# Scan layer: six convolution tiles projected in 512-column matmuls over both halves of x

## The chip, the core and the metric

The kernel runs on one core of a Trainium2 chip. Five engines of that core matter here: PE (TensorE, the matmuls), DVE (VectorE), ACT (ScalarE), POOL (GpSimd) and SP, which issues most of the transfers. Each engine works through its own list of instructions in order and waits on semaphores where an instruction needs another engine's result. The metric is the device time of one execution in microseconds (us); smaller is better. Three runs of the kernel before lie between 1007.13 and 1008.31 us.

## What is computed

The whole kernel is a decoder trunk of two layers on 256 tokens with 1024 channels. Each layer is FFN, mixer, FFN, with a layer norm after each; the first layer's mixer is a sparse attention, the second's a scan (SSD). The change lies in the scan mixer alone, in its beginning:

```python
def ssd_mixer(x, w_in, conv_w, conv_b, dt_bias, a_log, d_skip, norm_g, w_out):
    z, xbc, dt = jnp.split(x @ w_in, [SSM_INNER, SSM_INNER + SSM_CONV_DIM], axis=-1)
    xbc_pad = jnp.pad(xbc, ((0, 0), (SSM_CONV - 1, 0), (0, 0)))
    conv = conv_b + xbc_pad[:, 0:seq] * conv_w[0]
    for k in range(1, SSM_CONV):
        conv = conv + xbc_pad[:, k:k + seq] * conv_w[k]
    xbc = jax.nn.silu(conv)
    xs, b_in, c_in = jnp.split(xbc, [SSM_INNER, SSM_INNER + SSM_GROUPS * SSM_STATE], axis=-1)
    ...
    y = ssd_scan(xs, dt, a, b_in, c_in)
```

`xbc` has 3072 columns: 2048 of xs (four groups of 512), 512 of B and 512 of C. All arithmetic is float32 in effect.

## The kernel before

**Split products.** The matmuls run in a rounded 32-bit format. To keep float32 accuracy a weight block is split into a high part `wh` (ACT casts it, line 326) and a low part `wl` (DVE subtracts the high part from the raw weights, line 354; for a few blocks ACT and a transfer of POOL make it, lines 332 and 333). The activations `xT` are split likewise and lie side by side in one tile, `xT.HL`: for each of eight blocks of 128 channels 256 columns of the high half `xT.H`, then 256 of the low half `xT.L`. A product is the sum of three: high by high, high by low, low by high.

**A convolution tile.** The 3072 columns are worked as 24 tiles of 128 channels by 256 tokens. `bc_tile` (line 1508) makes the four B tiles and the four C tiles, `xs_tile` (line 1622) those of the four groups of xs. Each calls `proj_b` (line 691), which issues 24 matmuls of 256 columns (lines 539, 540 and 541 in `mm3`, for eight blocks) into the first half of one PSUM bank, and then `conv` (line 1497):

- ACT writes `a` = bias + last tap times the bank (line 1500);
- `flush` lets ACT take the Silu of the tile before (line 1495), held back by one tile so that ACT need not wait for DVE;
- DVE adds the three other taps, each a SCALAR_TENSOR_TENSOR that reads the bank (line 1504);
- the tile's own Silu is put in the list `late` for the next call.

After that `W.pump` makes the next weight block or two: a cast on ACT, a subtraction on DVE. The bank comes from `xbank` (line 1460), three banks in turn.

**The order of the work.** It is written out by hand, at the end of `ssd`: the eight B and C tiles, with the cumulative sums of the decay behind the sixth (`cumsums`, line 1420: five small matmuls; then ACT loads its table for Exp, takes two exponentials and loads the table for Silu again); the four xs tiles of group 0, with `cb` behind the second; then `flush`, half of a z product (`z_half`, line 1466), `x_tok(0)`, and the groups.

In this document the tiles around the change are called C0 to C3 (the four C tiles) and X0 to X3 (group 0 of xs). Two places on PE need what `conv` made:

- `cb(0)`, `cb(1)` and `cb_cross` (lines 1519 to 1535), behind X1: three times four small matmuls on B and C, one for each head group (the profile counts each of them twice). Those of the fourth head group read C3's Silu. DVE then masks two results (line 1533, `cbm`) and ACT copies the third (line 1526, `cross`).
- `x_tok(0)` (line 1565), behind X3 and the z half: eight transposes (line 1570) of X0 to X3. The fourth reads X3's Silu.

`proj_w` (line 700) is used elsewhere, in the FFN (`one`, line 914): for each of the eight blocks one matmul of the high weights with all 512 columns of `xT.HL` (line 705), then for each block one of the low weights with the 256 high columns (line 707). The bank then holds high by low in its second half and the other two sums in its first; there ACT copies the second half out (line 929) and DVE adds the first to it (line 930).

Of the kernel before, what the change touches and what calls it, by code (L numbers as in the profile page):

```python
# [18 lines left out]
SEQ = 256  # L19
# [393 lines left out]
def trunk_kernel(ctx: ExitStack, tc: tile.TileContext, widths, forms, x, ln_g, ln_b, wts, kvg, convp,  # L413
                 dt_bias, a_log, d_skip, norm_g, out):
    nc = tc.nc
# [10 lines left out]
    def nm(s):  # L426
        cnt[0] += 1
        return f"{s}_{cnt[0]}"
# [7 lines left out]
    def f1(s):  # L436
        return wk.tile([128, 256], F32, name=nm(s), tag="f1", bufs=6)
# [10 lines left out]
    def pmm():  # L448
        return psum.tile([128, 512], F32, name=nm("pmm"), tag="pmm", bufs=2)
# [14 lines left out]
    W = Weights(nc, f4, ring, wts, widths, forms, SLOTS, RAWS)  # L464
# [73 lines left out]
    def mm3(ps, lh, ll, rh, rl, first, last, on=False):  # L538
        nc.tensor.matmul(ps, lh, rh, start=first, stop=False, skip_group_check=on)  # L539
        nc.tensor.matmul(ps, lh, rl, start=False, stop=False, skip_group_check=on)  # L540
        nc.tensor.matmul(ps, ll, rh, start=False, stop=last, skip_group_check=on)  # L541
# [149 lines left out]
    def proj_b(ps, xT, u, retire=True):  # L691

        H, L = W.get(u)
        for k in range(DK):
            c = slice(k * 128, (k + 1) * 128)
            mm3(ps, H[:, c], L[:, c], xT.H[:, k, :], xT.L[:, k, :], k == 0, k == DK - 1)
        if retire:
            W.retire(u + 1)

    def proj_w(ps, xT, u):  # L700


        H, L = W.get(u)
        for k in range(DK):
            nc.tensor.matmul(ps, H[:, k * 128:(k + 1) * 128], xT.HL[:, k, :], start=k == 0, stop=False)  # L705
        for k in range(DK):
            nc.tensor.matmul(ps[:, :SEQ], L[:, k * 128:(k + 1) * 128], xT.H[:, k, :], start=False, stop=k == DK - 1)
        W.retire(u + 1)

    def out_k(acc, t, lh, ll, u, first, last):  # L710
        H, L = W.get(u)
# [53 lines left out]
    def ffn(xT, u0, ln_i, first=False, last=False, ff=False, own=1, k1=5, mixer=False):  # L765
# [148 lines left out]
        def one(j):  # L914

            nonlocal u
            bank = pmm if j % 2 == 0 else ptr
            if j % 2 == 0:
                hH[j // 2], hL[j // 2] = r2("hH"), r2("hL")
            H, L = [a[j // 2][:, (j % 2) * 256:(j % 2 + 1) * 256] for a in (hH, hL)]  # L920
            g, h = f1("gate"), f1("h")

            def half(o):
                nonlocal u
                ps = bank()
                proj_w(ps, xT, u)
                W.product()
                u += 1
                nc.scalar.copy(o, ps[:, SEQ:])
                return lambda: nc.vector.tensor_add(o, ps[:, :SEQ], o)  # L930

            def mul():
                nc.vector.tensor_mul(h, h, g)
                W.owe(1400)
                later(lambda: nc.scalar.copy(H, h))
                later(lambda: nc.vector.tensor_sub(L, h, H.bitcast(F32)), 2)

            later(half(g))
            step(most=-1, plain=True)
            later(lambda: nc.scalar.activation(g, g, AF.Silu))  # L940
            later(half(h))
            later(mul, 2)
            step(most=-1, plain=True)
# [436 lines left out]
    def ssd(xT, u, ln_i):  # L1380
# [79 lines left out]
        def xbank():  # L1460

            turn[0] += 1
            return psum.tile([128, 512], F32, name=nm("pxs"), tag=("acc00", "acc01", "acc10")[turn[0] % 3], bufs=1)
# [29 lines left out]
        def flush():  # L1493
            while late:
                nc.scalar.activation(*late.pop(0), AF.Silu)

        def conv(ps, i, out_t, hold=False):
            w = convp_sb
            a = f1("cv")
            nc.scalar.activation(a, ps[:, :256], AF.Identity, bias=w[:, 4, i:i + 1], scale=w[:, 3, i:i + 1])  # L1500
            if not hold:
                flush()
            for s in range(1, 4):
                nc.vector.scalar_tensor_tensor(a[:, s:], ps[:, :256 - s], w[:, 3 - s, i:i + 1], a[:, s:],
                                               op0=ALU.mult, op1=ALU.add)
            late.append((out_t, a))

        def bc_tile(i):
            ps = xbank()
            proj_b(ps[:, :256], xT, u + 10 + i, False)  # L1510
            W.free(u + 10 + i)
            dst = bT if i < 4 else cTt
            conv(ps, 16 + i, dst[:, (i % 4) * 256:(i % 4 + 1) * 256])
            W.pump(1 + i % 2)

        cbm = f4("cbm")
# [105 lines left out]
        def xs_tile(g, i, uu, then=None):  # L1622
            if not i:
                xsT[g] = []
            ps = xbank() if g < 3 else pmm()
            proj_b(ps[:, :256], xT, uu, False)
            W.free(uu)
            o = wk.tile([128, 256], F32, name=nm("xsT"), tag="xsT", bufs=5)
            hold = g == 3 and then is not None
            conv(ps, g * 4 + i, o, hold)  # L1630
            xsT[g].append(o)
            if then:
                then()
            if hold:
                nc.scalar.activation(*late.pop(0), AF.Silu)
            W.pump(1)
# [30 lines left out]
        for i in range(8):  # L1667
            bc_tile(i)
            if i == 5:
                cumsums()  # L1670
                for t in range(2):
                    decay_load(t, 0)
        u += 18
        for i in range(4):
            xs_tile(0, i, u + i)
            if i == 1:
                cb(0)
                cb(1)
                cb_cross()
# [11 lines left out]
        for g in range(2):  # L1691
            v = u + 8 * g
            fill += [lambda g=g, i=i, v=v: xs_tile(g + 1, i, v + i, first_diag if (g, i) == (0, 2) else None)
                     for i in range(4)]
            fill += [lambda g=g, t=t, i=i, v=v: (z_half(g + 2, t, i, v + 4), t and i and decay(g + 1), W.pump(1))
                     for t in range(2) for i in range(2)]
        v = u + 16
        fill += [lambda i=i, k=k, x=x, v=v: xs_tile(3, k, v + i, (lambda: run2(1)) if k == 1 else None) if x else out_piece(k, v + i)
                 for i, (x, k) in enumerate(((1, 0), (1, 1), (0, 0), (1, 2), (1, 3), (0, 1), (0, 2), (0, 3)))]
        fill += [lambda i=i, v=v: out_piece(4 + i, v + 8 + i) for i in range(6)]  # L1700
# [72 lines left out]
    xT = XT(True)  # L1773
    u, xT = ffn(xT, 0, 0, first=True, mixer=True)
    u, xT = attention(xT, u, 1)
    u, xT = ffn(xT, u, 2, ff=True)
    u, xT = ffn(xT, u, 3, own=3, k1=4, mixer=True)
    u, xT = ssd(xT, u, 4)
    u, _ = ffn(xT, u, 5, last=True)
# [36 lines left out]
```

## Time and profile before

| | |
|---|---|
| median of 3 runs | 1007.43 us (1007.13 to 1008.31) |
| the profiled execution's own time | 1007.07 us |
| its span, first to last instruction | 1005.4 us |
| mean granted TensorE clock | 0.998 of full speed |
| PE busy in the span | 996.3 us (99%) |
| DVE busy | 903.4 us (90%) |
| ACT busy | 667.6 us (66%) |
| POOL busy | 110.7 us (11%) |
| mean DMA rate | 231 GB/s |
| stretch of the tiles C0 to X3 | about 668 to 698 us |

Each row of a timeline has the start of an instruction (or of a run of like ones) in us from the span's start, its duration, the engine, the line of the kernel, the operation with its output and inputs, and, in square brackets, how long the engine was idle before and what ended that. A run of n like instructions has "xn" behind it. Instructions of one engine overlap a little: what one costs its engine in a row of others is the distance to the next start. For matmuls this matters most, since their durations include the way through the array: a 256-column one is shown with 0.28 us, and the next starts 0.12 us later.

### The profile page before, as it was taken

How to read it: one execution, taken by the hardware profiler on the slowest of the kernel's cores; microseconds unless marked ns; L12 is line 12 of the kernel's file. 1: busy time of each engine (PE TensorE's matmuls, PEld its weight loads, DVE VectorE, ACT ScalarE, POOL GpSimd, SP SyncE). 2: the span in 40 equal slices, each digit the busy share in tenths (PEclk: the TensorE clock that was granted, in tenths of full speed). 3: DMA queues.
4: the chain of work that ended last, by engine and by line, in shares of the span. 5: the costliest groups of instructions: out<-in, count | busy, mean ns of one | idle time of the engine just before them, and what ended most of it. 6: DMA issues, size and time to landing. Idle time of an engine off the chain costs nothing.

```text
span 1005.4 us, 14633 instructions
## 1 busy us (share of the span) xinstructions
PE 996.3 (99%) x5305; PEld 842.1 (84%) x5305; DVE 903.4 (90%) x1222; ACT 667.6 (66%) x978; POOL 110.7 (11%) x151
## 2 busy tenths in 40 slices
PE   9999999999999999999999999999999999999997
PEld 6888888898788888888888888999888888888886
DVE  6899999889898999999899999788899988899996
ACT  6676776576755776764577776486778645676670
POOL 0010110100000101100010110251121110010100
PEclk9999999999999999999999999999999999999999
DMA  9699889651754998995499999657765754689981
GB/s 348 218 291 279 242 262 327 225 170 63 236 180 126 273 271 236 272 383 199 125 273 274 240 266 358 208 163 237 229 212 200 256 173 139 181 251 288 288 255 42
DMA packets 66343, 232.74 MB, mean 231 GB/s; under 512 B 8144, under 2 KB 9168, under 8 KB 66272
## 3 DMA queue, kind: packets, MB, share of 16 engines
q1 hardware_dynamic: 54288, 189.84, 51.9%
q0 software_dynamic: 11408, 41.46, 22.4%
q8 instruction: 41, 0.67, 0.3%
q10 hardware_dynamic: 576, 0.52, 0.2%
q14 instruction: 30, 0.25, 0.1%
HBM read 193.48 MB, written 1.08 MB: 194 GB/s over the span
## 4 chain that ended last, share of the span: by engine, by line
PE 97%; DMA 1%; DVE 1%; ACT 0%; issue 0%; DVEq 0%; ACTq 0%; SPq 0%
PE pmm L539 13%; PE pmm L541 13%; PE pmm L540 13%; PE acc L539 10%; PE acc L541 10%; PE acc L540 10%; PE ptr L540 2%; PE ptr L541 2%; PE ptr L539 2%; PE pxs L539 2%; PE pxs L540 2%; PE pxs L541 2%; PE pmm L705 1%; PE ptr L705 1%; PE ptr L797 1%; DMA raw<-in_wts_dram 1%
## 5 line engine op out<-in xcount | busy, mean ns | idle before, releaser
L354 DVE TENSOR_TENSOR wl<-raw,wh 128x1024 fp32r<-128x1024 f32 (+3 forms) x422 | 493.3, 1212 | 15.1 <-ACT wh L326 14.8
L326 ACT CAST wh<-raw 128x1024 fp32r<-128x1024 f32 (+2 forms) x431 | 428.9, 1043 | 94.9 <-DVE raw L293 49.1
L539 PE MATMUL acc<-wh,hH 128*128 128x512 f32 (+1 forms) x352 | 138.2, 393 | 0.0
L541 PE MATMUL acc<-wh,hL 128*128 128x512 f32 (+1 forms) x352 | 136.7, 388 | 0.0
L540 PE MATMUL acc<-wl,hH 128*128 128x512 f32 (+1 forms) x352 | 136.4, 388 | 0.0
L539 PE MATMUL pmm<-wh,xT 128*128 128x512 f32 (+2 forms) x304 | 118.9, 391 | 0.0
L541 PE MATMUL pmm<-wh,xT 128*128 128x512 f32 (+2 forms) x304 | 116.8, 384 | 0.0
L540 PE MATMUL pmm<-wl,xT 128*128 128x512 f32 (+2 forms) x304 | 116.6, 384 | 0.0
L266 POOL DMA_DIRECT2D raw<-raw x64 | 55.6, 869 | 490.6 <-DVE raw L293 261.0
L541 PE MATMUL pmm<-wh,xf 128*128 128x512 f32 x256 | 99.7, 390 | 0.0
L540 PE MATMUL pmm<-wl,xf 128*128 128x512 f32 x256 | 99.7, 389 | 0.0
L539 PE MATMUL pmm<-wh,xf 128*128 128x512 f32 x256 | 99.7, 389 | 0.0
L541 PEld LDWEIGHTS acc<-wh,hL 128*128 128x128 f32 x352 | 66.1, 188 | 13.6
L293 DVE TENSOR_TENSOR raw<-raw,raw 128x1024 f32<-128x1024 f32 x64 | 77.1, 1220 | 0.2
L540 PEld LDWEIGHTS acc<-wl,hH 128*128 128x128 f32 x352 | 66.2, 188 | 13.0
L539 PEld LDWEIGHTS acc<-wh,hH 128*128 128x128 f32 x352 | 66.2, 188 | 12.9
L541 PEld LDWEIGHTS pmm<-wh,xT 128*128 128x128 f32 x304 | 57.1, 188 | 11.6 <-DVE xT L536 0.2
L540 PEld LDWEIGHTS pmm<-wl,xT 128*128 128x128 f32 x304 | 57.2, 188 | 10.3 <-DVE wl L354 0.2
L539 PEld LDWEIGHTS pmm<-wh,xT 128*128 128x128 f32 x304 | 57.2, 188 | 10.0
L540 PEld LDWEIGHTS pmm<-wl,xf 128*128 128x128 f32 x256 | 48.1, 188 | 10.0
L539 PEld LDWEIGHTS pmm<-wh,xf 128*128 128x128 f32 x256 | 48.1, 188 | 10.0
L541 PEld LDWEIGHTS pmm<-wh,xf 128*128 128x128 f32 x256 | 48.1, 188 | 9.9
(338 smaller groups left out, 1785.1 us busy)
## 6 DMA issues: line engine op xcount, KB each, us to landing
raw<-in_wts_dram SPq DMA_DIRECT2D x338, 512.0 KB, 5.9
raw<-raw POOLq DMA_DIRECT2D x64, 512.0 KB, 5.7
M<-scr POOLq DMA_DIRECT2D x8, 512.0 KB, 6.5
wl<-raw POOLq DMA_DIRECT2D x7, 512.0 KB, 7.2
lng<-in_ln_g_dram SPq DMA_DIRECT2D x6, 512.0 KB, 5.1
lnb<-in_ln_b_dram SPq DMA_DIRECT2D x6, 512.0 KB, 5.6
raw<-in_wts_dram SPq DMA_DIRECT2D x4, 408.0 KB, 5.7
out_dram<-x SPq DMA_DIRECT2D x4, 256.0 KB, 2.1
```

The lines of the kernel that those rows point to most:

```text
L266: self.nc.gpsimd.dma_start(self.raw[r], self.raw[other], accum_op=ALU.add)
L293: self.nc.vector.tensor_add(self.raw[r], self.raw[r], self.raw[other])
L326: nc.scalar.copy(h[:, c:c + n], raw[:, c:c + n])
L354: self.nc.vector.tensor_sub(lo[:, s], raw[:, s], h[:, s].bitcast(F32))
L539: nc.tensor.matmul(ps, lh, rh, start=first, stop=False, skip_group_check=on)
L540: nc.tensor.matmul(ps, lh, rl, start=False, stop=False, skip_group_check=on)
L541: nc.tensor.matmul(ps, ll, rh, start=False, stop=last, skip_group_check=on)
L705: nc.tensor.matmul(ps, H[:, k * 128:(k + 1) * 128], xT.HL[:, k, :], start=k == 0, stop=False)
L797: nc.tensor.transpose(v[:, i, t * 128:(t + 1) * 128], hs[t][:, i * 128:(i + 1) * 128], ident)
```

## The change

`proj_w` gets a parameter so that it can leave the retiring of the weights to its caller. `conv` gets a parameter `wide`. Six tiles use both: C1, C2, C3 (`i > 4` in `bc_tile`) and X0, X1, X2 (`not g and i < 3` in `xs_tile`). For them `proj_w` fills a whole bank, with 8 matmuls of 512 columns and 8 of 256 in place of 24 of 256. `conv` then begins with an ACT copy of the bank's second half into the tile's output place, the flush of the tile before, and a DVE addition of the bank's first half; from there on the bias line (ACT) and the three taps (DVE) read that sum in SBUF, not the bank. All other tiles stay as they were.

```diff
-    def proj_w(ps, xT, u):
+    def proj_w(ps, xT, u, retire=True):
...
-        W.retire(u + 1)
+        if retire:
+            W.retire(u + 1)
...
-        def conv(ps, i, out_t, hold=False):
+        def conv(ps, i, out_t, hold=False, wide=False):
             w = convp_sb
             a = f1("cv")
+            if wide:
+                nc.scalar.copy(out_t, ps[:, SEQ:])
+                flush()
+                nc.vector.tensor_add(out_t, ps[:, :SEQ], out_t)
+                ps = out_t
             nc.scalar.activation(a, ps[:, :256], AF.Identity, bias=w[:, 4, i:i + 1], scale=w[:, 3, i:i + 1])
             if not hold:
                 flush()
...
         def bc_tile(i):
             ps = xbank()
-            proj_b(ps[:, :256], xT, u + 10 + i, False)
+            wide = i > 4
+            (proj_w if wide else proj_b)(ps if wide else ps[:, :256], xT, u + 10 + i, False)
             W.free(u + 10 + i)
             dst = bT if i < 4 else cTt
-            conv(ps, 16 + i, dst[:, (i % 4) * 256:(i % 4 + 1) * 256])
+            conv(ps, 16 + i, dst[:, (i % 4) * 256:(i % 4 + 1) * 256], wide=wide)
...
             ps = xbank() if g < 3 else pmm()
-            proj_b(ps[:, :256], xT, uu, False)
+            wide = not g and i < 3
+            (proj_w if wide else proj_b)(ps if wide else ps[:, :256], xT, uu, False)
...
-            conv(ps, g * 4 + i, o, hold)
+            conv(ps, g * 4 + i, o, hold, wide)
```

On DVE, from the two weight subtractions behind C0's tile to the second tap of C2, the list before has this (`wl` is a low weight part, `cv` the tile's running sum, `pxs` the bank, `at` and `nacs` what DVE takes from the cumulative sums):

```order
L354 TENSOR_TENSOR wl_6625<-raw_6542,wh_6624 128x1024 [waits DMAHW5_49,PE_49]
L354 TENSOR_TENSOR wl_6628<-raw_6583,wh_6627 128x1024 [waits DMAHW6_49,PE_49]
L1504 SCALAR_TENSOR_TENSOR cv_6697<-pxs_6672,convp_sb,cv_6697 128x255 [waits Activation_49]
L1504 SCALAR_TENSOR_TENSOR cv_6697<-pxs_6672,convp_sb,cv_6697 128x254 [waits DVE_49]
L1504 SCALAR_TENSOR_TENSOR cv_6697<-pxs_6672,convp_sb,cv_6697 128x253 [waits DVE_49]
L1430 COPY at_6716<-ptr_6708 32x256 [waits PE_49,Activation_49]
L1434 TENSOR_SCALAR nacs_6719<-ptr_6708 128x32
L1434 TENSOR_SCALAR nacs_6721<-ptr_6708 128x32
L1504 SCALAR_TENSOR_TENSOR cv_6752<-pxs_6727,convp_sb,cv_6752 128x255 [waits Activation_49]
```

and now, at the same place (line 1504 is the new addition here, 1510 the taps):

```order
L354 TENSOR_TENSOR wl_6625<-raw_6542,wh_6624 128x1024 [waits DMAHW5_49,PE_49]
L354 TENSOR_TENSOR wl_6628<-raw_6583,wh_6627 128x1024 [waits DMAHW6_49,PE_49]
L1504 TENSOR_TENSOR cTt_6242<-pxs_6672,cTt_6242 128x256 [waits Activation_49]
L1510 SCALAR_TENSOR_TENSOR cv_6689<-cTt_6242,convp_sb,cv_6689 128x255 [waits Activation_49]
L1510 SCALAR_TENSOR_TENSOR cv_6689<-cTt_6242,convp_sb,cv_6689 128x254 [waits DVE_49]
L1510 SCALAR_TENSOR_TENSOR cv_6689<-cTt_6242,convp_sb,cv_6689 128x253 [waits DVE_49]
L1431 COPY at_6710<-ptr_6702 32x256 [waits PE_49,Activation_49]
L1435 TENSOR_SCALAR nacs_6713<-ptr_6702 128x32
L1435 TENSOR_SCALAR nacs_6715<-ptr_6702 128x32
L1504 TENSOR_TENSOR cTt_6242<-pxs_6721,cTt_6242 128x256 [waits Activation_49]
L1510 SCALAR_TENSOR_TENSOR cv_6738<-cTt_6242,convp_sb,cv_6738 128x255 [waits Activation_49]
```

An addition stands ahead of the taps of each wide tile, behind the weight subtractions of the tile before, and both the addition and the first tap wait for ACT.

On ACT, from C1's tile to C2's, the list before has this (`dend` and `eacs` are the exponentials of the cumulative sums, `cTt` takes the Silu of the C tiles):

```order
L1500 ACTIVATE cv_6697<-pxs_6672,convp_sb 128x256 [waits PE_49]
L1495 ACTIVATE cTt_6242<-cv_6655 128x256 [waits DVE_49,Activation_49]
L326 CAST wh_6705<-raw_6622 128x1024 [waits DMAHW0_49]
L1427 ACT_TABLE_LOAD
L1427 ACTIVATE dend_6239<-ptr_6708 128x32 [waits PE_49]
L1428 ACTIVATE eacs_6240<-ptr_6708 128x32
L1500 ACTIVATE cv_6752<-pxs_6727,convp_sb 128x256 [waits PE_49]
L1495 ACT_TABLE_LOAD [waits DVE_49]
```

and now:

```order
L1502 COPY cTt_6242<-pxs_6672 128x256 [waits PE_49]
L1496 ACTIVATE cTt_6242<-cv_6655 128x256 [waits DVE_49,Activation_49]
L1506 ACTIVATE cv_6689<-cTt_6242,convp_sb 128x256 [waits DVE_49]
L326 CAST wh_6699<-raw_6622 128x1024 [waits DMAHW0_49]
L1428 ACT_TABLE_LOAD
L1428 ACTIVATE dend_6239<-ptr_6702 128x32 [waits PE_49]
L1429 ACTIVATE eacs_6240<-ptr_6702 128x32
L1502 COPY cTt_6242<-pxs_6721 128x256 [waits PE_49]
L1496 ACT_TABLE_LOAD [waits DVE_49]
L1496 ACTIVATE cTt_6242<-cv_6689 128x256 [waits Activation_49]
L1506 ACTIVATE cv_6738<-cTt_6242,convp_sb 128x256 [waits DVE_49]
```

The bias line (1506) now stands behind the Silu of the tile before, and it waits for DVE where it waited for PE; the cast and the table loads stand behind it.

## The prediction

> **What bounds the kernel now.** I read the page first. The span, and the shares of the chain of work that ended last:
>
> ```profile
> span 1005.4 us, 14633 instructions
> ...
> PE 97%; DMA 1%; DVE 1%; ACT 0%; issue 0%; DVEq 0%; ACTq 0%; SPq 0%
> ```
>
> The end is set by PE, so a time saved on PE is gained, and a time that PE waits is lost. The waits of PE come next; the longest in the whole span:
>
> ```profile
> PE ptr L492 <- DVE half L483: 1.2, 1, 1.2
> ```
>
> That is at the very start. Where the change lies PE waits for nobody. How near the others are to it is seen in the busy times of the stretches around the six tiles (columns: PE, PEld, DVE, ACT, POOL, then granted clock and DMA share):
>
> ```profile
> 675.00:687.00 12.00, 12.00 (x101) 11.85 (x100) 11.32 (x21) 10.79 (x17) 2.67 (x4) 1.00 0.81 216
> 687.00:699.00 12.00, 12.00 (x95) 11.46 (x93) 8.57 (x15) 7.11 (x14) 0.88 (x1) 1.00 0.82 255
> ```
>
> In the first, from C2 to X1, DVE has 0.68 us of 12 left and ACT 1.21. That is the number that matters most here: a change that gives both of them more to do has almost no cover.
>
> Then the timelines. PE's: one tile (X1), the twelve `cb` products behind it, and the transposes of `x_tok(0)`:
>
> ```profile
> 684.11 0.28 PE L539 MATMUL pxs<-xT,wh 128*128 128x256 f32 x1
> ...
> 686.99 1.06 PE L1532 MATMUL psp<-cTt,bT 128*128 128x128 f32 x8
> 687.89 1.06 PE L1532 MATMUL pmm<-cTt,bT 128*128 128x128 f32 x8
> ...
> 698.18 0.60 PE L1570 MATMUL py<-ident,xsT 128*128 128x128 f32 x4
> ```
>
> A tile takes 686.99 - 684.11 = 2.88 us, a set of four `cb` products 0.90. ACT's timeline from C1's cast to C2's, then the two Silus on which PE depends, C3's at 684.78 and X3's at 697.84:
>
> ```profile
> 675.59 1.04 ACT L326 CAST wh<-raw 128x1024 fp32r<-128x1024 f32 x1
> 676.64 1.28 ACT L1427 ACT_TABLE_LOAD   x1
> 677.93 0.20 ACT L1427 ACTIVATE dend<-ptr 128x32 f32<-128x32 f32 x1
> ...
> 678.55 0.56 ACT L1500 ACTIVATE cv<-pxs,convp_sb 128x256 f32<-128x256 f32 x1 [0.33 <-PE pxs L541]
> 679.14 1.28 ACT L1495 ACT_TABLE_LOAD   x1
> 680.43 0.42 ACT L1495 ACTIVATE cTt<-cv 128x256 f32<-128x256 f32 x1
> 680.75 1.03 ACT L326 CAST wh<-raw 128x1024 fp32r<-128x1024 f32 x1
> ...
> 684.78 0.41 ACT L1495 ACTIVATE cTt<-cv 128x256 f32<-128x256 f32 x1
> ...
> 697.84 0.42 ACT L1495 ACTIVATE xsT<-cv 128x256 f32<-128x256 f32 x1 [0.40 <-DVE cv L1504]
> ```
>
> C3's Silu ends at 685.19, and its readers start about 687.3 (the fourth of the set at 686.99): 2.1 us of cover. X3's ends at 698.26, when the transposes have begun and the fourth comes next: no cover at all.
>
> **PE's part.** A wide tile is priced by `proj_w` in the FFN:
>
> ```profile
> 846.26 1.98 PE L705 MATMUL pmm<-xT,wh 128*128 128x512 f32 x8
> 848.07 1.11 PE L707 MATMUL pmm<-xT,wl 128*128 128x256 f32 x8
> 849.04 2.11 PE L705 MATMUL pmm<-xT,wh 128*128 128x512 f32 x8
> ```
>
> 849.04 - 846.26 = 2.78 us, 0.10 under the 2.88. The columns streamed are the same 6144; only the cost of each instruction goes down. Six tiles would save 0.6 us. That is all that the change can gain.
>
> **The additions.** Six copies on ACT and six additions on DVE. The first row has ACT's price from the FFN, the others DVE's, from the groups with shapes kept apart:
>
> ```profile
> L929 ACT COPY gate<-pmm 128x256 f32<-128x256 f32 x4 | 1.5, 374 | 3.3 <-PE pmm L707 3.3
> ```
>
> ```profile
> L1504 DVE SCALAR_TENSOR_TENSOR cv<-pxs,convp_sb,cv 128x254 f32<-128x254 f32 x20 | 9.6, 482 | 0.7
> ...
> L1128 DVE SCALAR_TENSOR_TENSOR sc<-ridx,lt,sc 128x256 f32<-128x256 f32 x7 | 3.4, 485 | 0.3
> ...
> L930 DVE TENSOR_TENSOR gate<-pmm,gate 128x256 f32<-128x256 f32 x4 | 1.7, 418 | 0.0
> ```
>
> A copy is 0.37, an addition 0.42. The taps now read SBUF: line 1128 does the same operation from SBUF in 0.485 against 0.482 from the bank, so they keep their price. [...] The bias line from SBUF has no row of its own; I keep 0.56, and allow 0.1 either way.
>
> Beside the busy time comes a **new round trip**. Before, ACT's bias line waited for PE alone and could run while DVE was still at the weights; DVE found it ready. Now the addition stands in DVE's list behind the weight subtractions, ACT's bias line waits for it, and the taps wait for the bias line. In that time both engines stand still for each other, in every tile. DVE's list for a tile is addition, wait, taps, subtraction. The last two, and the masking behind `cb`, from DVE's timeline:
>
> ```profile
> 675.04 2.35 DVE L354 TENSOR_TENSOR wl<-raw,wh 128x1024 fp32r<-128x1024 f32 x2
> 677.31 1.51 DVE L1504 SCALAR_TENSOR_TENSOR cv<-pxs,convp_sb,cv 128x255 f32<-128x255 f32 x3
> 678.74 0.40 DVE L1430 COPY at<-ptr 32x256 f32<-32x256 f32 x1
> ...
> 689.88 0.69 DVE L1533 TENSOR_TENSOR cbm<-psp,tri 128x512 f32<-128x512 f32 x1 [0.57 <-PE pmm L1524]
> 690.48 0.68 DVE L1533 TENSOR_TENSOR cbm<-pmm,tri 128x512 f32<-128x512 f32 x1
> ```
>
> From start to start: a subtraction 1.14 (2.27 for two), three taps 1.43, a masking 0.60. For each handing over between engines I take 0.04, a choice that the range doubles. A tile's cycle is then addition 0.42 + 0.04, bias 0.56 + 0.04, taps 1.43, subtraction 1.14 = 3.63 us, where PE gives a new tile every 2.78.
>
> **The sum, step by step** (span time). C1's taps start at 677.31 in the trace, held by the two subtractions; its addition now starts there. Bias 677.77 to 678.33. Behind it stand ACT's cast (1.05 to the next start), the table load (1.29) and the two exponentials (0.2), so C2's copy comes at 680.87 and ends at 681.24; Silu's table 681.28 to 682.57, C1's Silu 0.32, C2's bias 682.89. Its taps 683.49, subtraction 684.92, C3's addition 686.06, bias 686.52, taps 687.12 (done 1.51 later), C3's Silu 688.67 to 689.08.
>
> PE comes to `cb` at 686.99 less five tiles' saving, 686.5, and has done three of the four head groups by 687.2 (0.90 for four). It waits until 689.1: **first wait, 1.9 to 2.2 us**.
>
> On DVE: C3's taps end by 688.55, subtraction, X0's addition 689.69, X1's 693.32 (one cycle). X1's part has the two maskings (1.20) in place of a subtraction: X2's addition 697.01. Its taps 698.07, subtraction 699.50, X3's taps 700.64 (its bias line, from the bank as before, is ready by then), Silu 702.19 to 702.61. Before it ended at 698.26: the transposes come 4.35 us later. From `cb` to the transposes PE worked 698.18 - 686.99 = 11.19 us; after its first wait it has that to do less the 0.68 done and the 0.10 saved on X2, and is there at 699.5. With the three transposes that it can do first (some 0.3) that makes a **second wait, some 2.9 us**. The two waits, 4.8 to 5.1, less the 0.6 saved make the same 4.2 to 4.5. The saving itself is lost: a PE that comes earlier only waits longer.
>
> Overlaps on ACT (a start comes up to 0.1 us before the end of the one before) take 0.2 off between C1 and C2: 4.1 to 4.35. I take **4.2**.
>
> What else moves. Casts behind the bias line come up to 4 us later, but each block is cast ahead: the one that is held at 678 belongs to the second tile of the next group, eight tiles on. Loads wait for raw tiles that DVE's subtractions set free, so they come as much later as the casts that need them, with the DMA share at 0.82. POOL and SP get no instruction. Banks come free with the addition: C2's at 681.7, well ahead of X1 at 683.7. After `x_tok(0)` everything is shifted alike, and PE sets the pace again, as the 97% say; nothing gives the 4.2 back.
>
> From the profiled execution's 1007.07 us that is 1011.3. The median of the runs shown is 1007.43, 0.36 above it, so 1011.6 against that; I predict 1011.5.
>
> **Rivals.**
> *Hidden, or a small gain.* The copies and additions fit beside PE and the 0.6 us is gained: 1006.8. For it: in 687 to 699 DVE has 3.4 us idle. Against it: the 0.68 us before that, and that the round trip cannot be filled by an engine that works its list in order. It holds only if a tile's cycle stays at 2.78 or below, or C3's Silu ends by 687.2 and X3's by 697.6, 5 us earlier than I work out. 0.10; this is the one on the other side.
> *Cheaper taps.* If a tap from SBUF took what the addition takes, 0.42 and not 0.48, fifteen taps in the chain (C2 to X2) give 0.9 back: 1010.6. [...] Rows 1128 and 1504 speak against it. 0.10.
> *A slower clock after the waits.* The granted clock is 1.00 in the windows here, but none of them has a PE idle for more than 1.2 us. If it halved for one tile after each wait, the first loss would vanish in the second wait, and the second would cost 2.9: 1014.4. [...] 0.05.
> *Half of it.* One of the two waits comes out much shorter, because DVE finds a bias line ready that I have as late: about 1009.4. 0.05.
>
> **How the numbers follow.** About 0.2%, 2.0 us, can be told from no change. The forecast has 0.70, and with the cheaper taps, the slower clock and most of the half case it makes slower by over 0.2% 0.88; same 0.10 (most of the hidden case, and the part of the half case that falls short of 1009.4); faster by over 0.2% 0.02, a rest of the hidden case, since 0.6 us is all that I see to gain. The range holds the forecast with its unknown prices (bias line 0.1 in five tiles, 0.5; handing over doubled in ten places, 0.4, on both sides together 0.9) and the cheaper taps with them: 1009.6 to 1013.0. It leaves out the hidden, the slower-clock and the half case, 0.20.
>
> **What would show it.** Right: in the profile after, PE idle in front of the `cb` products with ACT's `cTt` Silu as releaser, and again in front of the x_tok transposes with `xsT`, 2 to 3 us each; DVE idle some 0.6 us in each wide tile between addition and taps, with ACT's bias line as releaser; ACT idle until DVE's addition; additions 3.6 us apart from C3 on; wide tiles 2.8 us on PE. Wrong: PE without gaps between 670 and 705, or taps well under 0.48, or a PE that waits at a third place, for a weight or a bank.

## The result, and the profile after

| | before | after |
|---|---|---|
| median of the runs compared (6 each) | 1007.64 us | 1013.07 us |
| lowest to highest | 1007.13 to 1008.31 us | 1012.43 to 1014.00 us |
| ratio, 95% interval | | 1.0054 [1.0044, 1.0064] |
| profiled execution, its span | 1007.07 us, 1005.4 us | 1013.86 us, 1012.1 us |
| mean granted TensorE clock | 0.998 | 0.996 |

The change costs 5.4 us. The forecast was 1011.5 us with a range up to 1013.0; the median lies 0.07 us above that upper end.

The chain of work that ended last, from the page of after, has DVE and ACT in it now:

```profile
PE 88%; DVE 6%; DMA 2%; ACT 2%; issue 2%; POOL 0%; DVEq 0%; ACTq 0%; SPq 0%; POOLq 0%
```

The longest waits of PE in after (us in total, times, longest):

```profile
PE py L1577 <- ACT xsT L1496: 2.2, 1, 2.2
PE psp L1539 <- ACT cTt L1496: 1.8, 1, 1.8
PE ptr L492 <- DVE half L483: 1.2, 1, 1.2
PE pmm L685 <- ACT wh L326: 0.6, 1, 0.6
```

The first two are new, and they stand where the prediction put them: `cb` (line 1539) waits for C3's Silu, the transposes (line 1577) for X3's. The last is a start-up wait that before has too, shorter. PE's timeline of after shows the wide tiles and both waits:

```profile
679.11 2.00 PE L705 MATMUL pxs<-xT,wh 128*128 128x512 f32 x8
...
681.90 2.00 PE L705 MATMUL pxs<-xT,wh 128*128 128x512 f32 x8
...
690.08 0.49 PE L1539 MATMUL psp<-cTt,bT 128*128 128x128 f32 x2 [1.76 <-ACT cTt L1496]
...
700.61 0.85 PE L1577 MATMUL py<-ident,xsT 128*128 128x128 f32 x3
703.69 0.33 PE L1577 MATMUL py<-ident,xsT 128*128 128x128 f32 x1 [2.24 <-ACT xsT L1496]
703.86 0.60 PE L1577 MATMUL ptr<-ident,xsT 128*128 128x128 f32 x4
704.22 0.38 PE L539 MATMUL pxs<-xT,wh 128*128 128x256 f32 x1
704.41 0.39 PE L540 MATMUL pxs<-xT,wh 128*128 128x256 f32 x1
704.61 0.41 PE L541 MATMUL pxs<-xT,wl 128*128 128x256 f32 x1
```

A wide tile takes 681.90 - 679.11 = 2.79 us. The last rows hold something not foreseen: from 704.41 on the 256-column matmuls start 0.20 to 0.22 us apart, where it is 0.12 elsewhere. The windows of this stretch show why (columns: PE, PEld, DVE, ACT, POOL busy, granted clock, DMA share, GB/s):

```profile
700.00:704.00 4.00, 1.62 (x10) 1.03 (x9) 3.89 (x7) 2.54 (x5) 0.00 (x0) 1.00 0.33 56
704.00:705.00 1.00, 1.00 (x9) 1.00 (x7) 1.00 (x2) 0.98 (x2) 0.00 (x0) 0.71 0.85 291
705.00:706.00 1.00, 1.00 (x7) 1.00 (x6) 1.00 (x3) 0.99 (x2) 0.00 (x0) 0.50 1.04 418
...
707.00:708.00 1.00, 1.00 (x7) 1.00 (x7) 1.00 (x3) 0.00 (x0) 0.00 (x0) 0.58 0.07 20
708.00:709.00 1.00, 1.00 (x10) 1.00 (x10) 1.00 (x2) 0.04 (x1) 0.00 (x0) 1.00 0.00 0
```

The granted clock falls to 0.50 shortly after the second wait and comes back before 708. In the 40 slices of the profile's page, some 25 us each, no such stretch can be seen; only the mean, 0.996 for 0.998, hints at it.

**Where the 6.7 us of span went.** The same matmul in both traces, each ahead of, between or behind the places in question. In before:

```profile
644.25 0.49 PE L557 MATMUL ptr<-ident,x 128*128 128x128 f32 x3
...
698.61 0.60 PE L1570 MATMUL ptr<-ident,xsT 128*128 128x128 f32 x4
...
707.77 0.44 PE L1585 MATMUL ptr<-M,xdt 128*64 128x128 f32 x4
...
819.40 0.38 PE L557 MATMUL pxT<-ident,x 128*128 128x128 f32 x2
```

and in after:

```profile
645.19 0.38 PE L557 MATMUL ptr<-ident,x 128*128 128x128 f32 x2
...
714.52 0.44 PE L1592 MATMUL ptr<-M,xdt 128*64 128x128 f32 x4
...
826.15 0.49 PE L557 MATMUL pxT<-ident,x 128*128 128x128 f32 x3
```

At 645, ahead of every changed tile, after is already 645.19 - 644.25 = 0.94 us late. This is no part of the change: 0.36 is there at line 685's matmuls of the start (11.12 for 10.76), and ahead of 645 this execution has two more waits of PE of 0.2 us each that the one of before has not (line 540 for `wl`, line 557 for DVE's `x`). The fourth transpose comes at 703.69 for about 698.5 (the set of four starts at 698.18, the next one at 698.61), 5.2 late, so 4.25 from the two waits. At the next common matmul the lag is 714.52 - 707.77 = 6.75: another 1.56 in a stretch in which nobody waits and the clock is at half. From there it stays at 6.75 (826.15 against 819.40).

### The profile page after: what moved, and what is told of

Read it like the earlier page. It is cut to its first block, busy times and chain, and to the rows that moved or that the text cites. A ratio compares the mean times of both kernels' runs of the same rounds, so it can differ in the third digit from the quotient of the medians.

```text
span 1012.1 us, 14544 instructions
## 1 busy us (share of the span) xinstructions
PE 998.2 (99%) x5257; PEld 841.0 (83%) x5257; DVE 905.6 (89%) x1228; ACT 670.5 (66%) x984; POOL 110.5 (11%) x151
## 4 chain that ended last, share of the span: by engine, by line
PE 88%; DVE 6%; DMA 2%; ACT 2%; issue 2%; POOL 0%; DVEq 0%; ACTq 0%; SPq 0%; POOLq 0%
PE pmm L539 12%; PE pmm L540 12%; PE pmm L541 12%; PE acc L539 9%; PE acc L541 9%; PE acc L540 9%; DVE wl L354 3%; PE ptr L539 2%; PE ptr L541 2%; PE ptr L540 2%; PE pmm L705 1%; PE ptr L705 1%; PE ptr L798 1%; DVE cv L1510 1%; DMA raw<-raw 1%
```

## The experiments

All eight were compared with the kernel before on the same chip in the same hours. In the first four that one took 1007.76 us (13 runs, 1007.27 to 1008.30), in the last four 1007.64 us (33 runs, 1006.93 to 1008.88). The edits are to the kernel after, but for the fourth.

**1. The round trip taken away, the work kept.** The bias line reads the bank's first half and stands ahead of the addition, so that ACT waits for PE alone again. Copies, additions and wide matmuls stay. The bias line's tap leaves out the high-by-low products in the six tiles.

```diff
             if wide:
                 nc.scalar.copy(out_t, ps[:, SEQ:])
+            nc.scalar.activation(a, ps[:, :256], AF.Identity, ...)
+            if wide:
                 flush()
                 nc.vector.tensor_add(out_t, ps[:, :SEQ], out_t)
                 ps = out_t
-            nc.scalar.activation(a, ps[:, :256], AF.Identity, ...)
```

> Copy and addition stay in the six wide tiles, but ACT's bias line reads the bank's first half at once, ahead of the flush, and does not wait for DVE's addition. (So the last tap of these tiles leaves out the high-by-low products.) Theory, the round trip: DVE finds the bias line ready, its cycle falls from 3.63 to about 3.0 us, C3's Silu comes before PE needs it and X3's within some 0.5 us: no wait of 2 us on PE, no fall of the clock, 1007.0 to 1008.2 us. Rival, the added work itself (0.42 us of DVE and 0.37 of ACT in each tile where both were nearly full): the waits stay for the most part, 1010 us or more.

Measured: 1007.78 us (10 runs, 1007.35 to 1009.75), ratio 1.0003 [0.9993, 1.0013]. Both new waits are gone from PE's list, and DVE runs without a gap from C1's addition to the maskings behind `cb`. A part of its timeline:

```profile
683.76 0.42 DVE L1506 TENSOR_TENSOR cTt<-pxs,cTt 128x256 f32<-128x256 f32 x1
684.21 1.52 DVE L1511 SCALAR_TENSOR_TENSOR cv<-cTt,convp_sb,cv 128x255 f32<-128x255 f32 x3
685.65 1.22 DVE L354 TENSOR_TENSOR wl<-raw,wh 128x1024 fp32r<-128x1024 f32 x1
686.79 0.42 DVE L1506 TENSOR_TENSOR xsT<-pxs,xsT 128x256 f32<-128x256 f32 x1
```

From addition to addition it is 3.03 us, for the same instructions. The copies and additions, less what PE saves in the wide matmuls, change nothing that can be measured in the medians; the 5.4 us come with the waiting. The trace says a little more: from the transposes at 645 to the first product with `M` this kernel takes 63.29 us and before 707.77 - 644.25 = 63.52. So some 0.2 of the half microsecond that PE saves is left, and the other 0.3 is what six copies and additions still cost.

**2. PE kept busy through the second wait.** Nine 512-column matmuls whose result nobody reads, in front of `x_tok(0)`.

```diff
         z_half(1, 1, 1, uz)
+        pb = pmm()
+        for _ in range(9):
+            nc.tensor.matmul(pb, xT.HL[:, 0, :128], xT.HL[:, 0, :], start=True, stop=True)
         x_tok(0)
```

> The changed kernel with nine extra matmuls of 512 columns, whose result is not used, between the z half and the transposes of x_tok(0): PE has 2.0 us of work in the wait of 2.24 us. Theory, the clock falls because PE stood still: the granted clock stays at 1.00 from 703 to 708 us and the time falls by about 1.5 us, to 1011.4 to 1011.9. Rival, the 6.7 us in the span come from waits alone or from another place: no change, 1012.8 to 1013.4 us.

Measured: 1012.17 us (4 runs, 1011.99 to 1012.61), ratio 1.0044 [1.0029, 1.0059]: 0.3 above the span that I gave, in the median. PE's second wait is 0.5 us, and the stretch in which after has the half clock is at full clock here:

```profile
704.00:705.00 1.00, 1.00 (x9) 1.00 (x10) 1.00 (x2) 0.98 (x2) 0.00 (x0) 1.00 1.00 295
705.00:706.00 1.00, 1.00 (x10) 1.00 (x10) 1.00 (x2) 0.99 (x2) 0.00 (x0) 1.00 0.96 373
```

The added work runs in time that PE would have waited: the fourth transpose comes 58.50 us after the transposes at 645, as in after (703.69 - 645.19 = 58.50). What is left, 1012.17 - 1007.76 = 4.4 us, is the two places where PE has to wait. So the half clock hangs on PE's idleness there (0.5 us of wait in place of 2.24), not on what DVE and ACT do; nor do transfers explain it, since the DMA share is 1.00 and 0.96 here at full clock.

**3. The round trip without the wide matmuls.** The six tiles go back to 24 matmuls in half a bank; a copy and a DVE operation of the same cost stay (a maximum of the first half with its copy, which gives the same numbers).

```diff
-                nc.scalar.copy(out_t, ps[:, SEQ:])
+                nc.scalar.copy(out_t, ps[:, :SEQ])
                 flush()
-                nc.vector.tensor_add(out_t, ps[:, :SEQ], out_t)
+                nc.vector.tensor_max(out_t, ps[:, :SEQ], out_t)
...
-            (proj_w if wide else proj_b)(ps if wide else ps[:, :256], xT, u + 10 + i, False)
+            proj_b(ps[:, :256], xT, u + 10 + i, False)
```

(and the same line in `xs_tile`).

> The six tiles keep the 24 narrow matmuls; conv copies the bank to the output place on ACT and DVE takes the maximum of bank and copy (the same value), so copy and two-operand step cost what they cost in the change and every wait between ACT and DVE is the same. Theory, ACT and DVE set the end of both waits and the 0.6 us saved on PE is lost: the transposes come at the same time as in the changed kernel, PE's waits are together 0.6 us shorter, time 1012.4 to 1013.4. Rival, PE's saving is kept: 0.6 us more than the changed kernel, 1013.7.

Measured: 1013.66 us (4 runs), ratio 1.0058 [1.0043, 1.0073]. The time alone can't tell the two theories apart: 0.6 us stand against an interval of some 1.5 either way, and it lies where the rival had it. The trace can. PE's waits:

```profile
PE py L1577 <- ACT xsT L1496: 2.2, 1, 2.2
PE psp L1539 <- ACT cTt L1496: 1.3, 1, 1.3
```

and the place that counts, in its timeline:

```profile
644.67 1.03 PE L557 MATMUL ptr<-ident,x 128*128 128x128 f32 x8
...
703.16 0.47 PE L1577 MATMUL py<-ident,xsT 128*128 128x128 f32 x1 [2.23 <-ACT xsT L1496]
```

It is 0.42 late at 645 (644.67 against 644.25), so without that the fourth transpose comes at 702.74; in after it comes at 703.69 - 0.94 = 702.75. PE arrives later at `cb` here, waits less, and goes on at the same time. The 0.6 us of the wide matmuls are lost in the wait, as forecast. This kernel too has the half clock, and against the second experiment, in the same hour, with the same two places of the round trip, it is 1.5 us slower.

**4. A wait alone.** In the kernel *before*, nine ACT copies into a tile that nobody reads, in front of X3's flush: they hold up X3's Silu, and nothing else of the change is there.

```diff
+        dl = f1("dl")
+        for _ in range(9):
+            nc.scalar.copy(dl, cTt[:, :256])
         flush()
         decay_seg(0, 0)
```

> The kernel before with nine idle ACT copies ahead of X3's Silu, so that the fourth transpose of x_tok(0) waits some 2.3 us and nothing else is changed. Theory, a PE wait above 2 us lets the clock fall for some 3.4 us: a stretch at half clock behind the wait, in the profile, and 2.3 + 1.5 = 3.8 us, 1011.4. Rival, a wait costs only itself: 1009.9 and clock 1.00 throughout.

Measured: 1012.08 us in the median of four runs (1011.95, 1010.77, 1012.86, 1012.20), ratio 1.0041 [1.0026, 1.0056]. PE's wait came out longer than planned; its timeline, and the windows:

```profile
701.88 0.48 PE L1570 MATMUL py<-ident,xsT 128*128 128x128 f32 x1 [2.94 <-ACT xsT L1495]
```

```profile
701.00:702.00 1.00, 0.12 (x1) 0.13 (x2) 0.00 (x0) 0.97 (x4) 0.00 (x0) 0.85 0.91 373
702.00:703.00 1.00, 1.00 (x6) 1.00 (x6) 0.54 (x1) 0.98 (x2) 0.00 (x0) 0.50 0.02 8
...
705.00:706.00 1.00, 1.00 (x10) 1.00 (x10) 1.00 (x2) 0.00 (x0) 0.00 (x0) 0.94 0.00 0
```

One wait of 2.9 us gives +4.3. The half clock does not need the change, only the wait. And it does not come every time: the mean clock of the four runs is 0.996, 0.998, 0.996 and 0.996, and the run with 0.998 is 1010.77, which is +3.0, about the wait and nothing more. The other three are at +4.2 to +5.1.

**5 and 6. One half of the tiles each.** First C1, C2 and C3 wide and the xs tiles narrow:

```diff
-            wide = not g and i < 3
+            wide = False
```

> Only C1 to C3 are wide, X0 to X2 as before. Theory, a delay that runs up from tile to tile in the round trip: it is 3 cycles long and all there when PE comes to cb, so the first wait is as in the changed kernel (1.8 to 2.3 us); behind it the narrow tiles let DVE catch up and the second wait goes. Sum about +2.0 us, 1009.8, or 1010.8 in runs in which one wait of 2 us is enough to lower the clock. Rival, each wide tile costs the same 0.7 to 0.9 us wherever it stands: +2.5 to 2.9, and a part of it at x_tok(0).

then X0, X1 and X2 wide and the C tiles narrow:

```diff
-            wide = i > 4
+            wide = False
```

> Only X0 to X2 are wide, C1 to C3 as before. Theory, the delay starts at C1, where the addition is queued behind two subtractions and the bias line then holds ACT's table loads: without it the three X tiles start on time, meet the slack of the maskings, and leave a wait of some 0.7 us at x_tok(0) against 0.3 us saved: +0.3 us, 1008.0, clock 1.00. Rival, each wide tile costs the same wherever it stands: +2.5 us, 1010.2.

Measured: with the C tiles 1009.59 us, ratio 1.0019 [1.0009, 1.0028]; with the xs tiles 1007.83 us, ratio 1.0001 [0.9992, 1.0010] (10 runs each). PE's waits at the two places, of the first kernel and of the second:

```profile
PE psp L1539 <- ACT cTt L1496: 1.6, 1, 1.6
```

```profile
PE py L1577 <- ACT xsT L1496: 0.2, 1, 0.2
```

Three tiles of one kind cost 1.95 us, three of the other 0.2, six 5.4. So there is no price per tile. The C tiles bring PE into a wait because of C1: in the timelines its addition stands behind two subtractions, and two table loads stand behind its bias line (the eighth experiment leaves C1 out; which of the two counts for how much was not tested). In the xs tiles alone the delay ends nearly inside the cover; I had given their wait 0.7, and it was 0.2. Neither kernel's trace has a half clock in this stretch.

**7. The round trip filled.** The weight subtractions that are due are issued between addition and taps, so that DVE has work while ACT makes the bias line.

```diff
                 nc.vector.tensor_add(out_t, ps[:, :SEQ], out_t)
                 ps = out_t
+                W.lows()
```

> All six tiles stay wide. In conv the weight subtractions that are due anyway are issued right behind the addition, not after the taps: DVE then has 1.14 us of work while ACT makes the bias line, and a tile's cycle falls from 3.65 to 3.0 us. Nothing is left out. Theory, the round trip: a rest of about 1.8 us of wait at cb (C1's addition still stands behind two subtractions and its bias line ahead of the table loads) and 0.4 at x_tok(0), +1.5 us, 1009.2, clock 1.00 in most runs. Rival, the added work: unchanged, 1013.

Measured: 1009.10 us (10 runs), ratio 1.0015 [1.0006, 1.0024]. DVE's timeline of this kernel:

```profile
685.23 0.42 DVE L1504 TENSOR_TENSOR cTt<-pxs,cTt 128x256 f32<-128x256 f32 x1
685.57 1.22 DVE L354 TENSOR_TENSOR wl<-raw,wh 128x1024 fp32r<-128x1024 f32 x1
686.70 1.52 DVE L1511 SCALAR_TENSOR_TENSOR cv<-cTt,convp_sb,cv 128x255 f32<-128x255 f32 x3
688.13 0.42 DVE L1504 TENSOR_TENSOR xsT<-pxs,xsT 128x256 f32<-128x256 f32 x1
```

From C3 to X0 the cycle is 688.13 - 685.23 = 2.90 us in place of 3.66, and the same instructions cost 1.5 us, not 5.4. The gap is not filled everywhere: C1's and X1's tile find no subtraction due and keep a stand-still of 0.67 us. PE's waits are 1.0 at `cb` and 0.3 at the transposes; the clock stays at full.

**8. Filled, and C1 left out.** As the seventh, with `wide = i > 5`: C1, whose addition is the one behind two subtractions and ahead of the table loads, stays narrow.

```diff
+                W.lows()
...
-            wide = i > 4
+            wide = i > 5
```

> As filled, with C1 narrow: five wide tiles, C2, C3, X0, X1, X2. Theory: without C1 in front of the table loads no delay is carried into cb, the filled cycle of 3.0 us keeps up with PE for five tiles, and the 0.5 us that PE saves in five wide tiles is kept: -0.5 us, 1007.2. Rival, the cycle above 2.8 us still runs up 0.2 us a tile and is waited for at x_tok(0): 1007.7 to 1008.5.

Measured: 1007.17 us (11 runs, 1006.62 to 1007.97) against 1007.64, ratio 0.9995 [0.9986, 1.0003]. PE waits neither at `cb` nor at the transposes. Five tiles of some 0.09 us are 0.45, and 0.47 is what the medians differ by; in the trace the stretch from the transposes at 645 to the first product with `M` takes 63.09 us for 63.52. But the interval includes no change: it is the best of the versions run, and not shown to be better than before.

## Why the prediction came out as it did

**Right but for a hundredth or two: PE's saving, forecast as 0.10 us a tile.** Between other tiles the wide ones take 2.79 to 2.80 us, where 2.78 was forecast and before takes 2.88: 0.08 to 0.09 a tile, some 0.5 in all. Also right that it is lost (third experiment, by its trace).

**Right: the round trip as the mechanism.** DVE's and ACT's timelines of after show the three places at which they stand still for each other. DVE:

```profile
678.23 0.41 DVE L1504 TENSOR_TENSOR cTt<-pxs,cTt 128x256 f32<-128x256 f32 x1
679.31 1.52 DVE L1510 SCALAR_TENSOR_TENSOR cv<-cTt,convp_sb,cv 128x255 f32<-128x255 f32 x3 [0.67 <-ACT cv L1506]
...
686.91 0.42 DVE L1504 TENSOR_TENSOR cTt<-pxs,cTt 128x256 f32<-128x256 f32 x1
688.00 1.52 DVE L1510 SCALAR_TENSOR_TENSOR cv<-cTt,convp_sb,cv 128x255 f32<-128x255 f32 x3 [0.67 <-ACT cv L1506]
...
697.96 0.42 DVE L1504 TENSOR_TENSOR xsT<-pxs,xsT 128x256 f32<-128x256 f32 x1
```

ACT:

```profile
678.68 0.60 ACT L1506 ACTIVATE cv<-cTt,convp_sb 128x256 f32<-128x256 f32 x1 [2.12 <-DVE cTt L1504]
...
689.61 0.42 ACT L1496 ACTIVATE cTt<-cv 128x256 f32<-128x256 f32 x1 [0.44 <-DVE cv L1510]
...
703.22 0.42 ACT L1496 ACTIVATE xsT<-cv 128x256 f32<-128x256 f32 x1 [1.21 <-DVE cv L1510]
```

Less the 0.94 that this execution was late at 645, C1's addition is at 677.29 (forecast 677.31), C3's at 685.97 (686.06), X2's at 697.02 (697.01). The cycle is (697.96 - 686.91) / 3 = 3.68 us for 3.63; the step with two maskings is the longest of the three, the one from C3 to X0 is 3.66. C3's Silu ends at 690.03 - 0.94 = 689.09 (689.08), X3's at 703.64 - 0.94 = 702.70 (702.61 at the latest).

**Right in the sum, a little off apiece: the two waits.** The first is 1.76 for 1.9 to 2.2. The second is 2.24 for some 2.9 (2.8 by the forecast's own times): the view counts it from the end of the three transposes before it, which it shows with 0.85 us; I had given them 0.3, from start to start. From start to start, as the forecast counted, PE stands still for 1.9 us (690.08 - 687.49, less 0.68 for three sets of four) and 2.8 us (703.69 - 700.61, less 0.3): 4.7 together, 4.2 less the saving. What counts is when the fourth transpose starts: 4.25 late, for 4.1 to 4.35.

**Wrong: the rival "A slower clock after the waits", its chance and its size.** This is the step that failed. The prediction let the clock stay at full, gave the other case 0.05 and left it out of the range, so the sum holds nothing for it. That waits of 1.9 to 2.9 us leave the clock alone was an estimate of mine which no run showed. The clock did fall. In the profiled execution of after the fall costs 1.56 us on top of the 4.25. In the medians it is about 1.0 us: after stands 5.4 above before, the second experiment, where the clock stays at full, 4.4, and its 1012.17 us lies inside the range. The range was also wider upward than its own terms: 1011.5 + 0.9 is 1012.4, not 1013.0, so the near miss of 0.07 us is no measure of how near the sum was. The size given to the rival was off as well: not "one tile" of 2.9 us lost, but a stretch of 3.41 us at half clock, in which by my estimate 3.41 x 0.5 = 1.7 us of work is not done; the lag grew by 1.56. Nor did each wait do it: the windows from 690 to 704 show 1.00 behind the first wait of 1.76, and the waits of 1.6 (fifth experiment) and 1.0 (seventh) left no trace in the clock either. Those of 2.24, 2.23 and 2.94 did.

The kernel before has such a fall as well, at its very end, where no time hangs on it. This window of it is full clock for 0.14 us and half for the rest, so the clock goes to half at 1001.64, 3.48 us after PE's last matmul (998.16):

```profile
1001.50:1002.00 0.50, 0.00 (x0) 0.00 (x0) 0.50 (x2) 0.00 (x0) 0.00 (x0) 0.64 0.00 0
```

How long the fall lasts can be measured where PE goes on to work. In after the clock is at half from about 704.42 to 707.83, worked out from these two windows, which it shares between full and half:

```profile
704.25:704.50 0.25, 0.25 (x4) 0.25 (x3) 0.25 (x2) 0.25 (x1) 0.00 (x0) 0.84 1.15 410
...
707.75:708.00 0.25, 0.25 (x4) 0.25 (x3) 0.25 (x2) 0.00 (x0) 0.00 (x0) 0.83 0.00 0
```

(0.84 is full clock for 0.17 us of the first, 0.83 half clock for 0.08 us of the second). That is 3.41 us, and in the third and the fourth experiment the same working gives 3.41 too (703.18 to 706.59 and 701.70 to 705.11). In as long a stretch ahead of the fall PE was not idle throughout: it was busy for 1.05 us in after and 0.65 us in the fourth experiment (1.14 in the third):

```profile
701.01:704.42 3.41, 1.05 (x8) 0.87 (x9) 3.34 (x6) 2.18 (x5) 0.00 (x0) 1.00 0.31 62
```

```profile
698.29:701.70 3.41, 0.65 (x5) 0.32 (x3) 2.00 (x2) 3.19 (x9) 0.00 (x0) 1.00 1.01 389
```

Around PE's first wait of after, which brought no fall, it was busy for 1.65 us of as long a stretch:

```profile
687.36:690.77 3.41, 1.65 (x15) 1.46 (x14) 2.70 (x5) 2.22 (x4) 0.19 (x1) 1.00 0.87 258
```

After, too, has one more fall behind PE's last matmul, which ends at 1004.93. This window puts it at 1008.21, 3.28 us later:

```profile
1008.10:1008.60 0.50, 0.00 (x0) 0.00 (x0) 0.50 (x2) 0.00 (x0) 0.00 (x0) 0.61 0.00 0
```

From the beginning of PE's idle time to the fall it is thus 3.28 and 3.48 us at the ends of after and before, 2.97 us at the second wait of after (704.42, less 703.69 - 2.24), 2.25 in the third experiment (703.18, less 703.16 - 2.23) and 2.76 in the fourth (701.70, less 701.88 - 2.94): no fixed time, and in after PE was at work again for 0.73 us when the clock went down. What decides when it goes down, and why the fall comes in some runs of a kernel and not in others, was not shown.

How many of after's runs have the fall can be told from their mean clocks only, and not for certain: 0.996 or 0.997 in four of the six (0.997 also stands in 4 of the 33 runs of before), and 0.998 in the two of 1012.43 and 1012.76 us. The waits alone would give about 1007.64 + 4.25 = 1011.9; what the rest of these two is, no trace shows.

**The other rivals.** *Cheaper taps* falls: from SBUF three taps show 1.52 us, from the bank 1.51 (the running sum, their second input, lies in SBUF both times). *Hidden* falls with the waits; that it needed a cycle at or below PE's tile was the right condition: at 2.90 in the tiles that could be filled (seventh and eighth experiment) nearly everything fits. *Half of it* falls in after; the fifth experiment is what one wait alone costs. The bias line from SBUF, which had no row, takes 0.60 for 0.56. POOL, SP and the loads made no third wait.

## What to carry to other kernels

When a step is handed from one in-order engine to another and back, compare the whole cycle of a tile, the standing still included, with the time of the engine that sets the pace: here a cycle of 3.66 against 2.79 us, begun behind two subtractions and ahead of two table loads, cost 4.25 us over six tiles, and the same instructions without the round trip cost nothing that the medians show. If the round trip must stay, put work that is due anyway into the gap, and don't begin it behind a long instruction or ahead of table loads. A wait of PE like those of 2.24, 2.23 and 2.94 us here is not priced by its length alone: look in narrow windows behind it for a clock at half, and keep something for that in the range (1.56 us in after).

## What the runs showed of the hardware

- The granted clock fell to 0.50 for 3.41 us at PE's waits of 2.24, 2.23 and 2.94 us, and not in every run of the same kernel (fourth experiment: 1010.77 at a mean clock of 0.998, the others 1011.95 to 1012.86 at 0.996). Behind waits of 1.76, 1.6 and 1.0 us it stayed at 1.00. The fall came 2.25 to 2.97 us after PE's idle time began, and at the ends of after and before 3.28 and 3.48 us after.
- At half clock 256-column matmuls start 0.20 to 0.22 us apart (after, from 704.41 to 707.81), less than twice the 0.12 us at full clock.
- A 256-column tap costs DVE the same from SBUF as from a bank (1.52 and 1.51 us for three), a bias line costs ACT 0.04 us more from SBUF (0.60 and 0.56).
